# Second layer of a three-layer block: where the first weights and the modulation rows' operands are loaded

## The chip, the cores and the metric

One core of a Trainium2 chip runs the whole program. The time is device microseconds from start to end of one execution; the median of several runs is given, and one further execution is recorded by the hardware profiler. In the text TensorE is PE in the rows, VectorE DVE, ScalarE ACT, GpSimd POOL, and SP is the engine whose queue issues most of the DMAs.

## The reference, cut to what matters

Three layers run one after the other on a sequence of 1024 tokens of width 1024: a layer with two kinds of attention, a layer with latent attention (the one that is edited), and a block whose norms are scaled and shifted by modulation rows, with a mixture of experts at its end. Everything is float32. Of the second layer this is what is computed first:

```python
def mla_layer(x, norm_g, w_in, q_norm, w_uq, kv_norm, w_ukv, w_o, cos, sin):
    h = rms_norm(x, norm_g)
    proj = h @ w_in                                   # 1024 -> 384 + 256 + 32 + 1024
    q_lat, kv_lat, k_rope, gate = split_cols(proj, L1_SIZES)
    q = (rms_norm(q_lat, q_norm) @ w_uq)              # 384 -> 16 heads of 64 + 32
    kv = (rms_norm(kv_lat, kv_norm) @ w_ukv)          # 256 -> 16 heads of 64 + 64
    ...
    return x + (o * jax.nn.silu(gate)) @ w_o
```

The third block begins with

```python
mod = jnp.einsum('bd,de->be', c_act, w_ada[l]) + b_ada[l]
sh1, sc1, g1, sh2, sc2, g2 = [m[:, None, :] for m in jnp.split(mod, N_ADA, axis=-1)]
h = rmsnorm(x, norm_mix_g[l]) * (1.0 + sc1) + sh1
```

## The kernel before, in words

A float32 product is made of three TensorE passes: each operand is split into a rounded part (`_h`, a cast on ScalarE, line 134) and the rest (`_l`, a subtraction on VectorE, line 135), and `mm3` (lines 139 to 141) adds the three products that matter in one PSUM bank. So every weight is loaded to a raw tile, cast, subtracted, and only then used. `load_w` (line 209) does this; with `parts=2` it loads and splits the rows in two halves through one raw tile, so that the second half's DMA waits until the first half is split. With `scale` (lines 227, 228) the split multiplies by a per-row gain.

The order on each engine is set when the program is built: a scheduler goes through the instructions in the order in which the code makes them and, by a model of their times, lets one go ahead whose operands come earlier. So the order on a queue isn't always that of the text. Tiles come from pools; a pool that is opened after another was closed takes the same memory, and the first use of a tile waits for the last use of the tiles that lay there. Most DMAs are issued on SP's queue, in order.

**The step in front** is `out_phase` (line 957), the end of the first layer: for each of 8 tiles of 128 tokens it multiplies by the output weights, adds to the row `x` (line 975), and calls `norm0` (line 1918), which stores `x` (line 1921), norms it (`norm_to_T`, line 246: the normed rows `xn` by VectorE at line 250, eight transposes by TensorE at line 261, the split at lines 134 and 135) and so writes tile t of the hidden state `hT`. Its tiles lie in the pool `c0`.

**The second layer** (`layer1`, line 1034) then opens the pool `lt` in the same memory. It loads the first group of the latents' weights (224 columns of `o_w_in`, tile `wl`, raw tile `wlraw`), then the value weights (`rwv`, lines 1064 to 1078: loaded once for the sum of squares that gives a scale, line 1067, and again to be scaled and split, lines 1076 and 1077). The latents are made in three groups of 224 columns by eight tiles of tokens: `project(c, t)` (line 1081) issues 24 matmuls into one of three PSUM banks, ScalarE sums squares from the bank (line 1085) and VectorE copies it to `lat` (line 1087). The next group's weights are loaded at tile 0 of a group. In the third group `finish(t)` norms and transposes the latents of a tile, and `values(t - 1)` makes the values, which SP stores to `v_d` (line 1125).

When `lt` is closed the pools `w1`, `pq1` (staging of the outputs) and `rq1` follow in its memory. The rotary tables `cosT` and `sinT` are loaded (lines 1145, 1146), and four rounds `c` each load query weights (`wq`, 384 by 256), make two blocks of queries, load key weights (`wk`, 256 by 256), and make two blocks of keys; the first two rounds also make the rotary parts (`rotary`).

Attention follows, head by head (line 1209 and after). Other work is dealt out between its steps by hand: gates up to head 7, half products of the output (`poh`) from head 9 on, bias rows, and from head 5 on in every second step one call of `mod2.run(1, mp)`, which is `total` (line 1306) of `ada_rows`. A modulation row of 1024 is made in four pieces of 256 columns; 24 pieces in all. Their partial sums, 128 rows by 256 columns, were stored to `part_d` long before (line 1304). `total` loads them to `adx` and the bias row to `mb`, sums over the 128 rows with a matmul of ones into the bank that the half products and gates use too, adds the bias, for two of the rows loads a gain into the same `mb` (line 1318) and multiplies, and stores the piece to `mod_d` (line 1320). `adx` and `mb` have one buffer each.

Of the kernel before, what the change touches and what calls it, by code (L numbers as in the profile page):

```python
# [11 lines left out]
F32 = mybir.dt.float32  # L12
# [4 lines left out]
AF = mybir.ActivationFunctionType  # L17
# [1015 lines left out]

def layer1(kk, ps, a, hT, hold, mix_d, gate_d, wo, mod, wx):

# [21 lines left out]
    with kk.pool(name="lt", bufs=1) as lt:  # L1057
        wl = [kk.load_w(lt, W, [(0, 224)], tag="wl", bufs=2, parts=2)]
        lat = lt.tile([P, NT, 672], F32, name="lat")
# [57 lines left out]
        def values(t):  # L1117
# [7 lines left out]
            nc.sync.dma_start(v_d[:, t], v16)  # L1125

        for c in range(3):
            for t in range(NT):
                if t == 0 and c < 2:
                    wl.append(kk.load_w(lt, W, [(224 * (c + 1), 224)], tag="wl", bufs=2, parts=2))  # L1130
                project(c, t)
                if c == 2:
                    finish(t)
                    if t:
                        values(t - 1)
        values(NT - 1)


# [5 lines left out]
    sinT = rq.tile([P, S], F32, name="sinT")  # L1144
    nc.sync.dma_start(cosT, a["c_cos"])
    nc.sync.dma_start(sinT, a["c_sin"])

# [26 lines left out]
    for c in range(4):  # L1174
        w = kk.load_w(wp, a["o_w_uq"], [(256 * c, 256)], nk=3, tag="wq", scale=gq)
        for j in range(2):
            proj_store(kk, ps, pq, w, j * P, P, qT, 3, qn_d, 256 * c + j * P)
        w = kk.load_w(wp, a["o_w_ukv"], [(256 * c, 256)], nk=2, tag="wk", scale=gk)
        for j in range(2):
# [97 lines left out]
def ada_rows(kk, ps, a, mod_d):  # L1277
# [27 lines left out]

    def total(s, z, dst, gname, ap_):
        o = s * D + z * H
        x = ap_.tile([P, H], F32, tag="adx", name=kk.nm("adx"))
        nc.sync.dma_start(x, part_d[:, o:o + H])
        b = ap_.tile([1, H], F32, tag="mb", name=kk.nm("mb"))  # L1310
        nc.sync.dma_start(b, a["b_ada_2"][:, o:o + H])
        pm = ps.tile([P, 512], F32, tag=MM_BANK[0], name=kk.nm("pm"), bufs=MM_BANK[1])
        nc.tensor.matmul(pm[0:1, :H], kk.ones[:, 0:1], x, start=True, stop=True)
        nc.vector.tensor_tensor(x[0:1, :], pm[0:1, :H], b, op=ALU.add)
        if dst == 5:
            nc.vector.tensor_scalar(x[0:1, :], x[0:1, :], 0.5, None, op0=ALU.mult)
        if gname:
            nc.sync.dma_start(b, a[gname][:, z * H:z * H + H])
            nc.vector.scalar_tensor_tensor(x[0:1, :], x[0:1, :], 1.0, b, op0=ALU.add, op1=ALU.mult)
        nc.sync.dma_start(mod_d[dst:dst + 1, z * H:z * H + H], x[0:1, :])  # L1320

    for s, dst, gname in ((1, 0, "norm_mix_g_2"), (0, 1, None), (2, 2, None), (4, 3, "norm_ffn_g_2"), (3, 4, None), (5, 5, None)):
        for z in range(D // H):
            u.add(lambda p, bufs, o=s * D + z * H: unit(o, p, bufs))
        for z in range(D // H):
            v.add(lambda p, s=s, z=z, dst=dst, gname=gname: total(s, z, dst, gname, p))
    return u, v
# [546 lines left out]
def tile_model(ctx: ExitStack, tc: tile.TileContext, a: dict, out: bass.AP, part=None):  # L1874
# [38 lines left out]
    r1 = rx.enter_context(kk.pool(name="r1", bufs=1, side="right"))  # L1913
    hT1 = HL(r1, full, "hT1", tag="hT")
    with kk.pool(name="c0", bufs=1) as op:
        gB = []

        def norm0(t, x):
            if t == 0:
                gB.append(bcast(kk, op, a["o_norm"], D, "gB1"))  # L1920
# [16 lines left out]
    wx = ExitStack()  # L1937
    layer1(kk, ps, a, hT1, hold, mix_d[1], gate_d[1], wo1, (totals, rows), wx)

# [230 lines left out]
```

## Time and profile before

| | |
|---|---|
| median of 3 runs (lowest, highest) | 2584.47 us (2582.06, 2587.52) |
| the profiled execution's own time | 2580.56 us |
| its span in the profile | 2578.8 us |
| TensorE (PE) busy | 2347.5 us, 91% |
| VectorE (DVE) busy | 1834.0 us, 71% |
| ScalarE (ACT) busy | 1379.5 us, 53% |
| GpSimd (POOL) busy | 439.5 us, 17% |
| DMA, mean | 203 GB/s |

Busy time counts an engine's instructions and not what it waits for, and a share over the whole span mixes stages with different limits; TensorE's busy time also grows when its clock is low. So the stages are read one by one, by the chain of work that ended last, the waits and the timelines. The step in front of the second layer ends at about 850 us, its latents and values are done at 963, queries and keys by about 1075, and its attention lasts from there to about 1475.

### The profile page before, as it was taken

Reading aid. Unit: us, or ns where it says so; the run is one execution under the profiler, and the core shown is the slowest. Engines: PE = TensorE matmul, PEld = TensorE weight load, DVE = VectorE, ACT = ScalarE, POOL = GpSimd, SP = SyncE. Lnnn points to the kernel's source line nnn. Section 1 sums busy time; section 2 is a strip of 40 time slices with the busy share of each in tenths; the row PEclk is TensorE's granted clock in tenths of the full one; section 3 lists DMA queues with packets and bytes.
Section 4 is the critical chain, followed back from the end, with each engine's and each line's share of the span. In section 5 each row is a group of like instructions: output and inputs, shape, how many; then the busy total and the mean of one; then the engine's idle time right before and its main releaser. Section 6 shows DMA issues by size and latency. Waiting matters only on the chain.

```text
span 2578.8 us, 41114 instructions
## 1 busy us (share of the span) xinstructions
PE 2347.5 (91%) x14476; PEld 1855.9 (72%) x14476; DVE 1834.0 (71%) x4607; ACT 1379.5 (53%) x2651; POOL 439.5 (17%) x626
## 2 busy tenths in 40 slices
PE   7988888998998888899989989989994999999998
PEld 6866655676787776688767767977873777777776
DVE  4459988876886355366776674767656888888886
ACT  4345675454662333255564466345452767776775
POOL 0000147766750012100000000011000101100110
PEclk9999888898999899999999989989996999999999
DMA  4442476565656226954776461544574999999994
GB/s 131 127 136 79 134 202 183 155 193 165 206 158 204 94 76 254 289 135 118 179 197 174 132 211 51 145 118 140 172 295 188 360 371 365 364 382 367 367 365 142
DMA packets 302637, 523.80 MB, mean 203 GB/s; under 512 B 46022, under 2 KB 191582, under 8 KB 302432
## 3 DMA queue, kind: packets, MB, share of 16 engines
q1 hardware_dynamic: 287456, 467.70, 55.6%
q0 software_dynamic: 14976, 53.49, 6.6%
q8 instruction: 114, 1.87, 0.3%
q14 instruction: 91, 0.75, 0.1%
HBM read 405.18 MB, written 115.65 MB: 202 GB/s over the span
## 4 chain that ended last, share of the span: by engine, by line
PE 61%; DMA 15%; DVE 11%; issue 4%; POOL 4%; ACT 3%; SPq 1%; POOLq 0%; DVEq 0%; ACTq 0%
PE sb L139 6%; PE sb L140 6%; PE sb L141 6%; PE sb L293 5%; DMA adw<-w_ada 4%; PE ptp L340 3%; PE w_gate L1816 2%; PE w_down L139 2%; PE w_down L141 2%; PE w_down L140 2%; PE w_up L1816 2%; DVE tkj L397 2%; PE w_gate L139 2%; PE w_gate L141 2%; PE w_gate L140 2%
## 5 line engine op out<-in xcount | busy, mean ns | idle before, releaser
L341 ACT CAST pTh<-ptp 128x512 f16<-128x512 f32 (+2 forms) x316 | 166.3, 557 | 135.6 <-PE ptp L340 130.1
L342 DVE TENSOR_TENSOR pTl<-ptp,pTh 128x512 f16<-128x512 f32 (+2 forms) x316 | 200.0, 648 | 39.8 <-ACT pTh L341 39.2
L1684 DVE TENSOR_TENSOR ring_l<-mraw,ring_h 128x1024 fp32r<-128x1024 f32 x170 | 203.8, 1221 | 27.6 <-ACT ring_h L1683 27.1
L1683 ACT CAST ring_h<-mraw 128x1024 fp32r<-128x1024 f32 x170 | 174.6, 1047 | 52.9 <-PE w_up L141 22.4
L1684 DVE TENSOR_TENSOR ring_l<-xraw,ring_h 128x1024 fp32r<-128x1024 f32 x150 | 180.2, 1221 | 24.6 <-ACT ring_h L1683 24.0
L340 PE MATMUL ptp<-ident,e 128*128 128x128 f32 x1184 | 182.2, 285 | 5.3 <-ACT e L1574 1.5
L1683 ACT CAST ring_h<-xraw 128x1024 fp32r<-128x1024 f32 x150 | 154.7, 1048 | 40.4 <-PE w_up L141 19.3
L340 PEld LDWEIGHTS ptp<-ident,e 128*128 128x128 f32 x1184 | 133.3, 144 | 18.1 <-issue 4.6
L1247 ACT ACTIVATE e<-e,nmx 128x1024 f32<-128x1024 f32 (+7 forms) x128 | 98.4, 771 | 72.5 <-DVE nmx L1245 72.3
L352 PEld LDWEIGHTS <-pTl 128*128 128x128 f16 x1184 | 107.8, 99 | 35.1 <-issue 16.1
L350 PEld LDWEIGHTS <-pTh 128*128 128x128 f16 x1184 | 109.6, 99 | 31.6 <-issue 21.2
L1773 POOL DMA_INDIRECT xg<-h_d,idx x16 | 24.0, 1501 | 589.8 <-DVE gate L1776 542.3
L1298 POOL TENSOR_SCALAR adw<-adw,ada_s 128x256 f32<-128x256 f32 x192 | 107.1, 569 | 98.8 <-DMA adw<-w_ada 98.3
L902 ACT ACTIVATE e<-e,nmx 128x1024 f32<-128x1024 f32 (+7 forms) x128 | 98.5, 771 | 45.6 <-DVE nmx L901 23.3
L351 PEld LDWEIGHTS <-pTh 128*128 128x128 f16 x1184 | 109.5, 99 | 3.8 <-issue 3.0
L139 PE MATMUL w_down<-ring_h,hTm_h 128*128 128x512 f32 x256 | 105.1, 411 | 0.0
L293 PE MATMUL sb<-hold_l,q 128*128 128x512 f32 (+3 forms) x384 | 102.5, 354 | 1.3 <-DMA q<-qr 1.3
L141 PE MATMUL w_down<-ring_h,hTm_l 128*128 128x512 f32 x256 | 101.1, 395 | 0.0
L140 PE MATMUL w_down<-ring_l,hTm_h 128*128 128x512 f32 x256 | 101.0, 395 | 0.0
L139 PE MATMUL pg<-hold_h,wg_h 128*128 128x512 f32 x192 | 84.7, 441 | 17.5 <-DVE gth L135 15.2
L317 DVE CUSTOM_DVE_ANT_0 e<-sb,hide 128x512 f32<-128x512 f32 (+3 forms) x128 | 74.5, 583 | 34.6 <-PE sb L293 20.6
L139 PE MATMUL w_up<-ring_h,xT_h 128*128 128x512 f32 x192 | 90.3, 470 | 0.0
(590 smaller groups left out, 7626.6 us busy)
## 6 DMA issues: line engine op xcount, KB each, us to landing
mraw<-w_up SPq DMA_DIRECT2D x35, 1024.0 KB
mraw<-w_gate SPq DMA_DIRECT2D x34, 1024.0 KB
mraw<-w_down SPq DMA_DIRECT2D x33, 1024.0 KB
xraw<-w_down SPq DMA_DIRECT2D x30, 1024.0 KB
xraw<-w_gate SPq DMA_DIRECT2D x30, 1024.0 KB
xraw<-w_up SPq DMA_DIRECT2D x29, 1024.0 KB
adw<-w_ada SPq DMA_DIRECT2D x96, 256.0 KB
xh_d<-hx SPq DMA_DIRECT2D x48, 256.0 KB
```

Of the source, the lines that this page charges most:

```text
L139: mm(out, a.hi, b.hi, start=start, stop=False)
L140: mm(out, a.hi, b.lo, start=False, stop=False)
L141: mm(out, a.lo, b.hi, start=False, stop=stop)
L293: mm(sc, a, b[:, k0:k0 + n], start=i == 0, stop=i == len(pairs) - 1)
L340: nc.tensor.transpose(pt[:, j, :], p[:, (g + j) * P:(g + j + 1) * P], kk.ident)
L341: nc.scalar.copy(hi[:, g:g + w, :], pt[:, :w, :])
L342: nc.vector.tensor_tensor(lo[:, g:g + w, :], pt[:, :w, :], hi[:, g:g + w, :], op=ALU.subtract)
L350: mm(out, hi[:, j, :], v1(off + j), start=j == 0, stop=False)
L351: mm(out, hi[:, j, :], v2(off + j), start=False, stop=False)
L352: mm(out, lo[:, j, :], v1(off + j), start=False, stop=j == nb - 1)
L1683: nc.scalar.copy(w.hi, raw_of(i))
L1684: nc.vector.tensor_tensor(w.lo, raw_of(i), w.hi.bitcast(F32), op=ALU.subtract)
```

## The change

The first group of the latents' weights is loaded and split in the step in front, at its tile 2, into tiles of a pool `early` that is opened on the other side of the memory, beside the hidden state, and closed after the last values. The second group is loaded at tile 2 of the first group into tiles of `lt`, the third at tile 2 of the second group into the tiles of `early`; each place holds one weight tile instead of two in `lt`. The first query weights are loaded and split by `queries()` at tile 1 of the third group, into a part of `hold` that is not in use then, through the raw tile of the latents' weights. In the rounds of queries and keys the key weights' load is issued ahead of the query products, and in the first round ahead of the rotary tables. `total` is cut in two: `fetch` issues the loads, with two buffers for `adx` and with the gain beside the bias in `mb`, and `total` of one piece calls `fetch` for the next at its end.

```diff
-def layer1(kk, ps, a, hT, hold, mix_d, gate_d, wo, mod, wx):
+def layer1(kk, ps, a, hT, hold, mix_d, gate_d, wo, mod, wx, wl, early, ex):
...
     with kk.pool(name="lt", bufs=1) as lt:
-        wl = [kk.load_w(lt, W, [(0, 224)], tag="wl", bufs=2, parts=2)]
         lat = lt.tile([P, NT, 672], F32, name="lat")
...
+        def queries():
+            raw = lt.tile([P, 4, 224], F32, tag="wl_raw", name=kk.nm("wqraw")).rearrange("p a b -> p (a b)")[:, 0:768].rearrange("p (k n) -> p k n", n=256)
+            w = HL.view(hold, lambda t: t[:, 5, 0:768].rearrange("p (k n) -> p k n", n=256))
+            nc.sync.dma_start(raw, a["o_w_uq"][:, 0:256].rearrange("(k p) n -> p k n", p=P))
+            for k in range(3):
+                h, l, s = w.hi[:, k, :], w.lo[:, k, :], gq[:, k:k + 1]
+                nc.scalar.activation(h, raw[:, k, :], AF.Copy, scale=s)
+                nc.vector.scalar_tensor_tensor(l, raw[:, k, :], s, h.bitcast(F32), op0=ALU.mult, op1=ALU.subtract)
+            return w
+
         for c in range(3):
             for t in range(NT):
-                if t == 0 and c < 2:
-                    wl.append(kk.load_w(lt, W, [(224 * (c + 1), 224)], tag="wl", bufs=2, parts=2))
+                if t == 2 and c < 2:
+                    wl.append(kk.load_w(early if c else lt, W, [(224 * (c + 1), 224)], tag="wl", parts=2))
+                if (c, t) == (2, 1):
+                    wq0 = queries()
                 project(c, t)
...
         values(NT - 1)
+    ex.close()
...
-    nc.sync.dma_start(cosT, a["c_cos"])
-    nc.sync.dma_start(sinT, a["c_sin"])
...
     for c in range(4):
-        w = kk.load_w(wp, a["o_w_uq"], [(256 * c, 256)], nk=3, tag="wq", scale=gq)
+        w = kk.load_w(wp, a["o_w_uq"], [(256 * c, 256)], nk=3, tag="wq", scale=gq) if c else wq0
+        wk = kk.load_w(wp, a["o_w_ukv"], [(256 * c, 256)], nk=2, tag="wk", scale=gk)
+        if c == 0:
+            nc.sync.dma_start(cosT, a["c_cos"])
+            nc.sync.dma_start(sinT, a["c_sin"])
         for j in range(2):
             proj_store(kk, ps, pq, w, j * P, P, qT, 3, qn_d, 256 * c + j * P)
-        w = kk.load_w(wp, a["o_w_ukv"], [(256 * c, 256)], nk=2, tag="wk", scale=gk)
+        w = wk
...
-    def total(s, z, dst, gname, ap_):
+    rows, loaded = [], {}
+
+    def fetch(i, ap_):
+        if i in loaded or i == len(rows):
+            return
+        s, z, dst, gname = rows[i]
         o = s * D + z * H
-        x = ap_.tile([P, H], F32, tag="adx", name=kk.nm("adx"))
+        x = ap_.tile([P, H], F32, tag="adx", name=kk.nm("adx"), bufs=2)
         nc.sync.dma_start(x, part_d[:, o:o + H])
-        b = ap_.tile([1, H], F32, tag="mb", name=kk.nm("mb"))
-        nc.sync.dma_start(b, a["b_ada_2"][:, o:o + H])
+        b = ap_.tile([1, 2, H], F32, tag="mb", name=kk.nm("mb"))
+        nc.sync.dma_start(b[:, 0], a["b_ada_2"][:, o:o + H])
+        if gname:
+            nc.sync.dma_start(b[:, 1], a[gname][:, z * H:z * H + H])
+        loaded[i] = x, b
+
+    def total(i, ap_):
+        fetch(i, ap_)
+        s, z, dst, gname = rows[i]
+        x, b = loaded[i]
         pm = ps.tile([P, 512], F32, tag=MM_BANK[0], name=kk.nm("pm"), bufs=MM_BANK[1])
         nc.tensor.matmul(pm[0:1, :H], kk.ones[:, 0:1], x, start=True, stop=True)
-        nc.vector.tensor_tensor(x[0:1, :], pm[0:1, :H], b, op=ALU.add)
+        nc.vector.tensor_tensor(x[0:1, :], pm[0:1, :H], b[:, 0], op=ALU.add)
...
         if gname:
-            nc.sync.dma_start(b, a[gname][:, z * H:z * H + H])
-            nc.vector.scalar_tensor_tensor(x[0:1, :], x[0:1, :], 1.0, b, op0=ALU.add, op1=ALU.mult)
+            nc.vector.scalar_tensor_tensor(x[0:1, :], x[0:1, :], 1.0, b[:, 1], op0=ALU.add, op1=ALU.mult)
         nc.sync.dma_start(mod_d[dst:dst + 1, z * H:z * H + H], x[0:1, :])
+        fetch(i + 1, ap_)
...
     hT1 = HL(r1, full, "hT1", tag="hT")
+    wl = []
+    ex = ExitStack()
+    early = ex.enter_context(kk.pool(name="wl0", bufs=1, side="right"))
...
         def norm0(t, x):
+            if t == 2:
+                wl.append(kk.load_w(early, a["o_w_in"], [(0, 224)], tag="wl", parts=2))
             if t == 0:
...
-    layer1(kk, ps, a, hT1, hold, mix_d[1], gate_d[1], wo1, (totals, rows), wx)
+    layer1(kk, ps, a, hT1, hold, mix_d[1], gate_d[1], wo1, (totals, rows), wx, wl, early, ex)
```

## Rows read from the trace of the kernel before

Starts are microseconds from the start of the span. In a timeline row stand the start, the duration, the engine, the line, the operation with its output and inputs, and in brackets how long the engine had been idle before it and what ended that.

**Rows 1.** Chain that ended last, 800 to 1080 us, in order of time: start, length, what.

```profile
847.93 3.61 DMA wlraw<-o_w_in
...
859.71 3.45 DMA wlraw<-o_w_in
...
965.10 6.12 DMA wqraw<-o_w_uq
```

**Rows 2.** Waits of TensorE, 842 to 1080 us: total in us, times, longest.

```profile
PE sb L139 <- ACT wq_h L227: 9.8, 1, 9.8
...
PE pt L261 <- DVE xn L250: 5.0, 2, 3.6
```

**Rows 3.** Timeline of TensorE around the first latents.

```profile
843.15 1.32 PE L261 MATMUL pt<-ident,xn 128*128 128x128 f32 x8 [1.38 <-DVE xn L250]
848.05 1.94 PE L261 MATMUL pt<-ident,xn 128*128 128x128 f32 x8 [3.58 <-DVE xn L250]
852.79 0.56 PE L139 MATMUL sb<-wl_h,hT_h 128*128 128x224 f32 x1 [2.80 <-ACT wl_h L134]
...
868.04 0.37 PE L139 MATMUL sb<-wl_h,hT_h 128*128 128x224 f32 x1 [3.42 <-DVE lat L1087]
```

**Rows 4.** Stretches: length, busy us (instructions) of PE, PEld, DVE, ACT, POOL, clock, DMA, GB/s.

```profile
800.00:834.00 34.00, 34.00 (x177) 28.51 (x177) 28.16 (x65) 12.62 (x23) 0.00 (x0) 1.00 0.63 208
...
845.60:859.20 13.60, 8.21 (x36) 7.57 (x36) 5.42 (x11) 5.54 (x8) 0.00 (x0) 0.50 0.65 224
869.50:872.80 3.30, 3.30 (x18) 3.30 (x17) 1.09 (x1) 0.76 (x3) 0.00 (x0) 0.50 0.18 26
890.00:900.00 10.00, 10.00 (x92) 10.00 (x91) 2.57 (x5) 3.01 (x21) 0.00 (x0) 1.00 0.01 2
...
965.10:975.20 10.10, 3.39 (x8) 2.72 (x9) 2.32 (x7) 2.10 (x5) 0.00 (x0) 0.50 0.70 222
1050.00:1060.00 10.00, 10.00 (x45) 8.06 (x44) 2.52 (x5) 2.35 (x4) 2.82 (x6) 1.00 0.69 257
1205.00:1475.00 270.00, 250.39 (x2396) 196.91 (x2394) 193.60 (x541) 145.42 (x308) 0.00 (x0) 0.98 0.61 164
```

**Rows 5.** Timeline of SP's queue after the last values.

```profile
963.40 0.34 SPq L1125 DMA_DIRECT2D v_d<-v  x1
...
964.26 0.79 SPq L1146 DMA_DIRECT2D sinT<-c_sin  x1
...
965.65 0.49 SPq L220 DMA_DIRECT2D wkraw<-o_w_ukv  x1
```

**Rows 6.** Waits of TensorE, 1205 to 1475 us: total in us, times, longest.

```profile
PE pm L1313 <- DMA adx<-ada_d: 13.8, 9, 2.9
PE pm L1313 <- DVE hx L948: 1.6, 1, 1.6
```

**Rows 7.** Tile `wlraw`: its casts and subtractions, ns shortest, median, longest, first and last start.

```profile
L134 ACT CAST wl_h<-wlraw x6: 929/940/942, 851.8 to 889.3; 128x896 fp32r<-128x896 f32 x6
L135 DVE TENSOR_TENSOR wl_l<-wlraw,wl_h x6: 1091/1092/1094, 852.8 to 890.2; 128x896 fp32r<-128x896 f32 x6
```

**Rows 8.** Timeline of VectorE, 863 to 871 us.

```profile
864.16 1.09 DVE L135 TENSOR_TENSOR wl_l<-wlraw,wl_h 128x896 fp32r<-128x896 f32 x1 [2.89 <-ACT wl_h L134]
865.21 2.48 DVE L1077 SCALAR_TENSOR_TENSOR hold_l<-rwv,gks,hold_h 128x1024 fp32r<-128x1024 f32 x2
867.61 0.98 DVE L1087 COPY lat<-sb 128x224 f32<-128x224 f32 x3
869.84 1.09 DVE L135 TENSOR_TENSOR wl_l<-wlraw,wl_h 128x896 fp32r<-128x896 f32 x1 [1.26 <-ACT wl_h L134]
```

**Rows 9.** The sums' matmuls: ns shortest, median, longest, first and last start.

```profile
L1313 PE MATMUL pm<-adx,ones x48: 376/377/634, 1211.5 to 1464.6; 128*1 128x256 f32 x48
```

**Rows 10.** Waits of SP's queue, 1205 to 1475 us: total in us, times, longest.

```profile
SPq L1309 <- DMA mod_d<-adx: 31.9, 21, 4.0
```

**Rows 11.** The partial sums' tile in memory: us from a DMA's issue to its landing.

```profile
DMA to landing us min/median/max: 2.0/3.3/7.1
```

More of the change, by code (lines that the diff above doesn't have):

```diff
@@ L1325, in ada_rows @@
         for z in range(D // H):
-            v.add(lambda p, s=s, z=z, dst=dst, gname=gname: total(s, z, dst, gname, p))
+            v.add(lambda p, i=len(rows): total(i, p))
+            rows.append((s, z, dst, gname))
     return u, v
```

## The prediction

> **What bounds the kernel now.** I read the page first (TensorE is busy nine tenths of the span, the table above), then the chain that ended last around the code that is edited, then TensorE's waits in the same stretches, then the timelines of the engines and of SP's queue at each gap. What the reader should see is that TensorE stands still, or runs at its lower clock, in three places that the edit touches, and hardly anywhere else nearby.
>
> First place, the start of the second layer. The chain leaves TensorE after the last transposes of the step in front and runs through the load of the latents' weights, its casts, the second group's load and the copy of a latent out of PSUM [rows 1]. TensorE's waits there are 5.0 us for the last normed rows [rows 2], 2.8 us for the first cast and 3.4 us for the copy of a latent out of PSUM [rows 3]. The timeline gives the positions: the first latent matmul starts at 852.79, seventy-two matmuls (three PSUM banks of 24) are issued, and the seventy-third starts only at 868.04 [rows 3]. At full clock 92 such matmuls go into 10 us [rows 4], so the seventy-two are 7.8 us of work and took 15.3 us.
>
> Second place, the first queries: one wait of 9.8 us for the cast of their weights [rows 2]. Their load goes out at 965.10 and needs 6.1 us [rows 1], because on SP's queue it comes behind the values' store and two rotary tables [rows 5].
>
> Third place, the second layer's attention from its sixth head on. TensorE is busy 250.4 of 270 us there, VectorE 193.6, ScalarE 145.4 [rows 4]. TensorE's longest wait by far is 13.8 us, nine times, in the sum over a modulation row's partial sums (line 1313), for their load; the next is 1.6 us [rows 6].
>
> **The clock** is part of each price. In 845.6 to 859.2, 869.5 to 872.8 and 965.1 to 975.2 the granted clock is 0.50, the 1.2 GHz level, each time after a gap in TensorE's work; in the attention stretch the mean is 0.98 of 2.4 GHz [rows 4].
>
> **A. Latents.** Removed: the first group's load from the start of the layer (two halves, each 3.6 us to land, 0.94 us of cast on ScalarE, 1.09 us of subtraction on VectorE [rows 1, 7]). It stood there because its raw tile shared memory with the step in front and was asked for at 847.93, the moment that step's last normed row was done. With the weights in tiles of their own, TensorE can start on tiles 0 to 5 of the hidden state while it waits for tiles 6 and 7. Between its transposes it is free for 3.6 us before 848.05 and 1.4 us before 843.15 [rows 3]: 5.0 us, or 45 matmuls. The transposes end at 850.0; the 27 that are left of the three banks take 2.9 us, to 852.9. That is 15.1 us before 868.04. The second low-clock stretch (3.4 us at half speed, 1.7 us lost) has no cause left: upper bound 16.8 us. Moving the second group's load from tile 0 to tile 2 also matters: now VectorE does that group's subtraction at 864.16 and the value weights' at 865.21 before it copies the first latent [rows 8], and the PSUM banks stay full that long.
> Lower bound: the copies still stand behind the value weights on VectorE. Their own loads can't start before 847.9 (same memory); 3.6 us to land, two squares (2.7), 2.0 for the scale, a second load (3.6), and two casts and subtractions (2.2 to the first, 1.3 to the second, overlapped) end near 862. Then the gain is 6.0 + 1.7 = 7.7 us. I take 14 us. It is nearer to the upper end because the queues are not in the order of the text: in [rows 8] a subtraction that is written after the value weights' runs before them, so work goes where its operands are expected.
>
> **B. First queries.** Their load, three casts and three subtractions move into the third group of latents, into the buffer half that nothing uses there. TensorE goes from the last value matmul straight to the queries: 9.8 us, and of the low clock in 965.1 to 975.2 the 3.4 us after 971.8 in which it worked cost 1.7: upper bound 11.5 us. What is late next is the key weights. Now issued fourth at 965.65, they go first, right behind the store at 963.40 [rows 5]; an estimate of 3.6 us as for the latents' half, and some 1 us of splitting, gives 968.5. The queries are 36 matmuls at 45 in 10 us [rows 4], 8 us, to 970.3: covered. If the keys' weights land as late as now, or the outputs' staging tiles must wait for the values' store, up to 4.5 us come back: lower bound 7. The rotary tables come after these loads and are wanted only after queries and keys, some 13 us on. I take 11 us.
>
> **C. Modulation rows.** 24 sums stand 11 us apart (1211.5 to 1464.6 over 23 steps [rows 9]). Before, the next load could not be issued until the previous row's store had landed: SP waited 31.9 us in 21 times for that [rows 10]. Now there are two buffers, and the load goes out right after the previous sum. A load lands in 2.0 to 7.1 us [rows 11], so 11 us cover even the longest. Gone: 13.8 us of TensorE, and 2% of 270 us, 5.4, if the clock holds: upper bound 19. Lower bound 2: the sum still shares one PSUM bank with the half products of the output (the 1.6 us row of [rows 6]), and VectorE, at 72%, may become what ends the next step. I take 13, the wait alone: the other waits of that list are near 1 us each, so little else is queued up behind it.
>
> **D. Costs.** The early group's 2.2 us of VectorE and 1.9 of ScalarE lie in a stretch where TensorE is busy 34.0 of 34.0 us and VectorE 28.2 [rows 4]; the 6 us that VectorE has left cover it. The queries' split adds 1.3 us to ScalarE in the third group. The second and third groups' loads start two tiles later and take 11 us (asked for at 859.71 [rows 1], split at 870.9 [rows 8]), against 16 us of matmuls left in the group. The number of DMAs is unchanged. On SP the second half of the early load waits for the first half's split, some 5.5 us, and the step's own loads and stores stand behind it; they are asked for a tile (6.8 us) ahead. 0 to 5 us; I take 2.
>
> **Sum:** 14 + 11 + 13 - 2 = 36 us. The profiled execution took 2580.56 us (span 2578.8 and 1.8 around it); 2544.6 after. The median shown is 3.9 us above that execution, so I forecast 2548.5.
>
> **The rivals.**
> R1, the latents start early but their copies stay behind the value weights: A is 7.7, the time 2554.8. For it: [rows 8]; against: the order there follows readiness.
> R2, the sums' wait only changes its name (the shared bank, VectorE): C is 2, the time 2559.5. For it: VectorE's 72%; against: the short list in [rows 6].
> R3, the early load holds up the step in front. Its halves take 3.6 us each [rows 1]; if the operands of a tile queue behind both, TensorE, which has no idle time there, loses up to 7.2 us once: 2555.7. The Trainium skill (DMA: Bandwidth & Descriptors, section Queues, rings and completion order) says that descriptors issued by SP are consumed in ring order on each DMA engine, which speaks against putting a large load there; no row before shows such a collision, and by this rule the sum would be 28.8 instead of 36.
> R4, the new tiles' memory is itself not free before the step in front ends, so that the load goes out at 847.9 as now: A is 1, the time 2561.5. Against: the side they are put on holds only the hidden state in that step.
> R5, slower. The prefetch is issued by SP right behind a sum, and its row of the bias has one buffer, so SP waits in order for VectorE; the next head's loads stand behind it. SP waited 1.5 us on average at this place before [rows 10] without TensorE losing time on head loads. If 24 such waits reach TensorE, C turns from 13 gained into 36 lost, 49 us against a gain of 36: 2597.5. It decides from 1 us per sum on (23 us from A, B and D over 24).
>
> **How the numbers follow.** Forecast 0.50, R1 0.20, R2 0.13, R3 0.05, R4 0.04: all faster, 0.92. R5 0.05. All parts given back by a changed order elsewhere, 0.03 for no change. "No change" means within 0.2%, 5.2 us, about what a measurement of this kernel can tell. The range takes all upper bounds (16.8 + 11.5 + 19 = 47.3 us) to all lower ones (7.7 + 7 + 2 - 5 = 11.7): 2537 to 2573, rounded down by 1 at each end. It holds the forecast and R1 to R4.
>
> **What would show it.** A: latent matmuls between the last transposes, none waiting for a cast of their weights, the granted clock at 1.00 where it was 0.50, the seventy-third near 853. B: no wait for the queries' cast, the first query matmul under 1 us after the last value matmul. C: no wait of line 1313 for its load. R3 would show as waits of the step in front for its operands, R5 as waits of the score matmuls for head loads. The prediction is wrong if the latents' copies or the staging tiles stop TensorE for over 10 us in the same stretches, or if attention keeps its 270 us.

## The result, and the profile after

The changed kernel takes 2552.07 us (median of 4 runs, 2548.09 to 2557.46); the kernel before, measured beside it, 2583.26 us (4 runs). The ratio is 0.9882, with a 95% interval of 0.986 to 0.9903. Measured once more on another occasion ("again", below) it is 0.9864 (0.9844 to 0.9883); one run of the kernel before took 2704.14 us there at a lower clock and is not counted. So some 31 to 35 us are gone, 36 were forecast, and the forecast of 2548.5 us is 3.6 us below the median. The parts did not come out as forecast, though; that is what the rest is about.

The page of the changed kernel, first part: busy time, share of the span (2550.8 us) and instructions of each engine.

```profile
PE 2337.4 (92%) x14476; PEld 1848.9 (72%) x14476; DVE 1836.8 (72%) x4607; ACT 1378.5 (54%) x2651; POOL 443.6 (17%) x626
```

TensorE's busy time is 10 us less than before, although it has the same matmuls to do: part of the work now runs at the higher clock (mean granted clock 0.952 in this execution, 0.947 before).

**The first latents.** TensorE's timeline of the changed kernel, where [rows 3] stood before:

```profile
831.27 1.04 PE L261 MATMUL pt<-ident,xn 128*128 128x128 f32 x8
832.06 0.35 PE L139 MATMUL sb<-wl_h,hT_h 128*128 128x224 f32 x1
...
840.49 0.60 PE L261 MATMUL pt<-ident,xn 128*128 128x128 f32 x4
841.03 0.60 PE L261 MATMUL pt<-ident,xn 128*128 128x128 f32 x4
...
843.39 0.37 PE L139 MATMUL sb<-wl_h,hT_h 128*128 128x224 f32 x1 [1.31 <-DVE lat L1086]
```

The first latent matmul (832.06) follows the transposes of the sixth tile at once, and the latents go on between the transposes of the last two tiles. The last transposes wait for nothing any more, and the seventy-third latent matmul (843.39) comes 2.0 us after the last transpose, where it came 18.5 us after it. All of TensorE's waits between 780 and 955 us:

```profile
PE sb L139 <- ACT hold_h L134: 4.6, 7, 0.7
PE ptl L1108 <- ACT lat L1092: 2.4, 2, 1.2
PE sb L139 <- DVE lat L1086: 1.3, 1, 1.3
PE sb L139 <- DVE pst_l L135: 1.0, 1, 1.0
PE sb L139 <- DVE v L1123: 0.5, 1, 0.5
```

The waits for the normed rows and for the weights' cast [rows 2, 3] are not in this list. The stretches of the changed kernel, with the columns of [rows 4]:

```profile
832.06:843.39 11.33, 10.02 (x92) 9.83 (x90) 7.75 (x18) 5.36 (x15) 0.00 (x0) 1.00 0.55 173
843.39:887.00 43.61, 41.80 (x369) 41.34 (x370) 18.60 (x54) 18.16 (x62) 2.29 (x12) 1.00 0.20 61
887.40:890.80 3.40, 3.40 (x16) 3.23 (x15) 0.67 (x3) 0.61 (x1) 0.00 (x0) 0.50 0.00 0
...
955.70:959.10 3.40, 3.40 (x8) 2.74 (x9) 2.24 (x5) 1.12 (x2) 0.53 (x1) 0.50 0.72 236
976.00:983.00 7.00, 3.50 (x8) 2.81 (x9) 1.98 (x3) 0.66 (x2) 1.11 (x2) 0.51 1.00 404
```

The granted clock is 1.00 through the first two groups of latents, where it was 0.50 twice; 3.4 us at 0.50 come in the third group. In the queries and keys the low clock has not gone: its stretches lie elsewhere than before.

**Queries and keys.** TensorE's waits from 936 to 1065 us in the changed kernel:

```profile
PE sb L139 <- DVE pst_l L135: 12.2, 5, 5.9
PE pg L139 <- DVE gth L784: 3.7, 2, 3.0
```

The 9.8 us for the queries' weights [rows 2] are gone. In their place stands a wait for a staging tile's subtraction, 12.2 us; in the same stretch the kernel before lost 6.7 us to it. ScalarE's timeline shows what is late behind it:

```profile
945.41 1.56 ACT L134 CAST pst_h<-sb 128x512 fp32r<-128x512 f32 x3 [3.88 <-DMA v_d<-v]
...
952.57 1.07 ACT L134 CAST pst_h<-sb 128x512 fp32r<-128x512 f32 x2 [2.83 <-DMA qn_hi<-pst_h]
...
975.00 1.07 ACT L134 CAST pst_h<-sb 128x512 fp32r<-128x512 f32 x2 [1.50 <-DMA qr<-qrs_h]
980.00 0.59 ACT L134 CAST pst_h<-sb 128x512 fp32r<-128x512 f32 x1 [3.93 <-DMA qr<-qrs_h]
```

Each block of queries or keys is cast into one of two staging tiles and stored from there (by GpSimd's queue, not SP's). The rotary rows (`qrs`) go through the same two tiles and are stored to `qr`. The first cast waits for the values' store (the tiles lie in the same memory), the later ones for the stores of what was in their tile before: the block two before at 952.57, the rotary rows at 975.00 and 980.00.

**Attention.** TensorE's waits from 1185 to 1470 us, where [rows 6] stood, and below it the wait of SP's queue that answers to [rows 10]:

```profile
PE pt L1010 <- DMA mxt<-mix_d: 4.5, 1, 4.5
PE pv L352 <- DVE pTl L342: 4.1, 4, 2.1
PE ptp L340 <- ACT e L1262: 3.7, 1, 3.7
PE pv L350 <- ACT pTh L341: 2.2, 3, 1.1
PE pm L1342 <- DVE brs L800: 1.3, 1, 1.3
PE pm L1342 <- DMA adx<-ada_d: 1.0, 1, 1.0
```

```profile
SPq L1329 <- DMA mod_d<-adx: 34.4, 18, 3.4
```

The wait for the partial sums fell from 13.8 to 1.0 us, but other waits, 14.5 us in all by the first four lines, now stand in the list; of the same kinds the kernel before had 2.7 us in its attention and 0.5 us (`mxt`) right behind it. Of these, the score matrix's exponentials (`e`), their casts (`pTh`) and the rest (`pTl`) are the attention's own chain through ScalarE and VectorE; `mxt` is the first operand of the closing step, which waits for the last head's store. The attention did not get shorter: from head 5's product with the values to the last head's last product it takes 250.8 us, 247.9 before. What fills it is work that used to follow (below).

### The profile page after: what moved, and what is told of

It is laid out like the page before. It is cut to its first block, busy times and chain, and to the rows that moved or that the text cites. A ratio compares the mean times of both kernels' runs of the same rounds, so it can differ in the third digit from the quotient of the medians.

```text
span 2550.8 us, 41148 instructions
## 1 busy us (share of the span) xinstructions
PE 2337.4 (92%) x14476; PEld 1848.9 (72%) x14476; DVE 1836.8 (72%) x4607; ACT 1378.5 (54%) x2651; POOL 443.6 (17%) x626
## 4 chain that ended last, share of the span: by engine, by line
PE 62%; DMA 14%; DVE 11%; issue 5%; POOL 4%; ACT 3%; SPq 1%; POOLq 0%; DVEq 0%; ACTq 0%
PE sb L139 6%; PE sb L140 6%; PE sb L141 6%; PE sb L293 5%; PE ptp L340 3%; DMA adw<-w_ada 3%; PE w_gate L1846 2%; PE w_down L139 2%; PE w_down L141 2%; PE w_down L140 2%; PE w_up L1846 2%; DVE tkj L397 2%; PE w_gate L139 2%; PE w_gate L141 2%; PE w_gate L140 2%
## 5 line engine op out<-in xcount | busy, mean ns | idle before, releaser
L340 PE MATMUL ptp<-ident,e 128*128 128x128 f32 x1184 | 181.0, 284 | 12.1 <-ACT e L1262 3.7
```

Of the source, the lines that this page charges most:

```text
L340: nc.tensor.transpose(pt[:, j, :], p[:, (g + j) * P:(g + j + 1) * P], kk.ident)
```

## The experiments

The program's first layer and its third block run at a clock that varies from execution to execution (the low-clock time of the first layer alone was 91 to 116 us), so a profiled execution's total says little about a few us. The table therefore gives, beside the ratio of the times to the kernel before (measured side by side; the quotient of the two medians differs from it by up to 0.0011), three stretches of each profiled execution: S1, from the last transpose of the step in front to the last latent matmul; S2, from there to the first head's product with the values; S3, from head 5's to the router of the third block, with TensorE's idle time in it (length less busy time). All are read from timelines and stretches. In the expectations, the "last normed rows' transposes before the second layer" are those of the sixth tile, the 831.27 above.

| kernel | ratio to before (95%) | S1 | S2 | S3 | idle in S3 |
|---|---|---|---|---|---|
| before | 1 | 102.9 | 148.7 | 660.5 | 53.3 |
| a_only: part A alone | 0.9924 (0.9902, 0.9946) | 85.4 | 152.4 | 655.7 | 52.0 |
| a_t0: A, later loads at tile 0 | 0.9937 (0.9914, 0.9961) | 85.5 | 151.8 | 662.8 | 54.0 |
| b_only: part B alone | 0.9983 (0.9971, 0.9995) | 102.6 | 145.9 | 660.8 | 53.7 |
| b_st0: B and a third staging tile | 0.9951 (0.9931, 0.9971) | 105.4 | 139.0 | 652.8 | 51.3 |
| c_only: part C alone | 0.9971 (0.9956, 0.9986) | 105.9 | 151.0 | 653.8 | 48.4 |
| c_buf: C's second buffers alone | 0.9983 (0.9964, 1.0003) | 102.2 | 151.6 | 655.6 | 48.1 |
| the changed kernel | 0.9882 (0.986, 0.9903) | 87.1 | 146.4 | 659.0 | 48.9 |
| again: the same | 0.9864 (0.9844, 0.9883) | 85.4 | 149.2 | 648.8 | 49.2 |
| a_held: early load held back | 0.9875 (0.9849, 0.9901) | 85.4 | 140.1 | 655.4 | 47.9 |
| s_pad: staging tiles elsewhere | 0.9888 (0.9869, 0.9906) | 85.5 | 149.1 | 652.8 | 47.3 |
| s_st0: a third staging tile | 0.9881 (0.9862, 0.9899) | 85.5 | 143.1 | 651.3 | 47.9 |
| tail: half products held back | 0.9922 (0.9906, 0.9938) | 85.5 | 146.8 | 658.0 | 49.0 |
| best: held load, third tile | 0.9897 (0.9873, 0.9921) | 85.4 | 144.4 | 653.5 | 48.8 |

The stretches scatter too. S2 is 148.7 to 152.4 us in the five kernels without part B (mean 151.1), though their code there is the same, and S1 is 102.2 to 105.9 in the five without part A.

**The three parts alone.** Each is the kernel before with that part of the diff.

> The first group of latents' weights early, and the later groups' loads at tile 2; queries and modulation rows as before. Theory (the parts add up; A is worth what the trace shows between the last transposes and the second group): from the end of the step in front to the 193rd latent matmul 16 to 17 us less than before, and all of the stretch from the last latent to the first head unchanged within 2 us; the whole 16 to 25 us less, by whether the 9 us that the changed kernel's trace shows less in the first layer come with this part (its order of work there is changed, because the load and its split went out near 605 us, in the first layer). Rival 1 (VectorE's copies stay late): under 8 us. Rival 2 (the first layer's 9 us are chance between two executions): 16 us less in time, and no lasting difference in the first layer.

> Only the first query weights' early split and the new order of loads in the first round. Theory from the changed kernel's trace: the wait of 9.8 us for the cast is gone, but about 7 us return as TensorE's wait for the subtraction into the staging tiles (12 us in that trace against 6.7 before), so 2 to 5 us less in the whole. Rival (as predicted, covered): 9 to 11 us less. Second rival (the return belongs to the combination with the latents' part): 9 us here too.

> Only the modulation rows' prefetch. As predicted: the 13.8 us of TensorE's waits gone and 13 us less in the whole. Theory from the changed kernel's trace: the waits for the load go from 13.8 to about 1 us, but TensorE's idle time from the sixth head to the router falls by only some 4 us, and the low-clock stretches there decide the rest: 0 to 6 us less. The first layer, whose order is the same as before, has the time of before; if its trace is again 5 us or more shorter, that difference is chance.

Measured: 0.9924, 0.9983 and 0.9971, that is about 20, 4 and 7 us. Their product, 0.9878, agrees with the changed kernel's two ratios within their intervals: the parts add. A shortens S1 by 17.5 us, B shortens S2 by 2.8, C takes 4.9 us out of TensorE's idle time in S3.

**The early load held back.** In the changed kernel the load stands in the code at tile 2 of the step in front, but the scheduler issued it at 604.7 us, in the first layer's attention, and with it changed the order of the instructions there. Here it is tied to the store of tile 1 on SP's queue, and it goes out at 802.1:

```diff
             if t == 2:
-                wl.append(kk.load_w(early, a["o_w_in"], [(0, 224)], tag="wl", parts=2))
+                with kk.tc.issue_after(gB[1]):
+                    wl.append(kk.load_w(early, a["o_w_in"], [(0, 224)], tag="wl", parts=2))
```

> The changed kernel, but the early load may not be issued on SP before the store of the rows of tile 1 of the step in front, so that the first layer's order is the same as before. If the first layer's 9 us come from the load's place in it, this kernel is 6 to 10 us slower than the changed one (ratio 0.991 to 0.993 against before instead of 0.988). If they are chance, it is as fast as the changed kernel within 3 us. If a load of 0.46 MB in the step in front holds up its operands (the rival of the prediction), TensorE's waits there grow by up to 7 us.

0.9875, and S1 as in the changed kernel: A's gain does not hang on the place of the load. With the load inside the step in front, TensorE's only waits from 785 to 863 us were these:

```profile
PE sb L139 <- ACT mT_h L134: 2.2, 1, 2.2
PE sb L139 <- DVE lat L1086: 1.5, 1, 1.5
```

None is for a load; the first comes at 785.72, ahead of the early load, and the second is that of the seventy-third latent matmul.

**The changed kernel again, and the tile of the later loads.** The second is part A alone with one character changed:

```diff
-                if t == 2 and c < 2:
+                if t == 0 and c < 2:
```

> The changed kernel itself, once more, so that the three kernels that go with it have it on the same chip. All theories: 0.988 of the kernel before, within 0.002. Its profile is a second look at the same program, and says what of the differences between profiled executions is chance: if the first layer again ends at 831 us (the last normed rows' transposes before the second layer), the 9.5 us by which it ended earlier than in the kernel before belong to the program; if it ends anywhere between 828 and 841, they are chance of the clock.

> Part A alone, but with the second and third group's weights loaded at tile 0 of a group as in the kernel before, not at tile 2; the first group's early load and the tiles of their own stay. Theory 1 (R1 of the prediction: what fills the start is decided by VectorE's order; a second group's split at tile 0 stands ahead of the latents' copies and stops TensorE when three banks are full): from the last normed rows' transposes to the seventy-third latent matmul it takes over 17 us instead of the 12.1 of part A alone (27.3 before), and the ratio is 0.994 to 0.9965 against 0.9924. Theory 2 (only the first group's early load matters; the scheduler places the later loads and splits by itself): 12 to 14 us, ratio 0.9915 to 0.9935.

In "again" the sixth tile's transposes come at 835.25: within the bounds for chance, which speaks against a gain of the full 9.5 us in the first layer. In a_t0 S1 is 85.5 us, the seventy-third latent matmul starts again 2.0 us after the last transpose (12.1 us after the sixth tile's transposes, as in a_only), and it waits for the same thing as in the changed kernel:

```profile
845.11 0.37 PE L139 MATMUL sb<-wl_h,hT_h 128*128 128x224 f32 x1 [1.31 <-DVE lat L1086]
```

On VectorE the copies of the first latents stand ahead of the value weights in both kernels; the scheduler puts them there whichever tile the load is written at. So the early first group, in tiles of its own, is all of A, and the move of the later loads is worth nothing that can be measured. The ratios (0.9937 and 0.9924) agree within their intervals.

**Staging tiles: place or number.** Two kernels made from the changed one. The first puts 5.5 KB of unused memory (in each of the 128 rows) ahead of the staging tiles; the second gives the first round a third tile.

```diff
     wp = px.enter_context(kk.pool(name="w1", bufs=2))
+    gap = px.enter_context(kk.pool(name="gap", bufs=1))
+    gap.tile([P, 1408], F32, name="gap")
```

```diff
+    s0 = rp.enter_context(kk.pool(name="st0", bufs=1))
...
-            proj_store(kk, ps, pq, w, j * P, P, qT, 3, qn_d, 256 * c + j * P)
+            proj_store(kk, ps, pq if c or j else s0, w, j * P, P, qT, 3, qn_d, 256 * c + j * P)
...
-            proj_store(kk, ps, pq, w, j * P, P, kT, 2, kn_d, 256 * c + j * P)
+            proj_store(kk, ps, pq if c or not j else s0, w, j * P, P, kT, 2, kn_d, 256 * c + j * P)
```

> The changed kernel with 5.5 KB of unused memory put between the weights' pool and the staging tiles of queries and keys, so that the first staging tiles no longer lie over the values' tiles; still two staging buffers. Theory 1 (part B is given back because the first staging cast waits 3.9 us for the values' store, and the queue of casts behind it slides): that wait is gone, TensorE's wait for the staging subtraction falls from 12.2 us to under 7.8, the stretch from the last latent matmul to the first head falls by 3 to 6 us, ratio 0.986 to 0.987. Theory 2 (it is given back because two staging buffers wait for their own stores of 2 to 3 us each, wherever they lie): TensorE's wait stays at 8 to 12 us, the stretch changes by less than 2 us, ratio as of the changed kernel within 0.001.

> The changed kernel with a third staging tile for the first round of queries and keys (first block of queries and second block of keys), in memory that the values' tiles do not touch. Theory 1 (place): the same as with the unused memory, 3 to 6 us less between the last latent matmul and the first head. Theory 2 (number of buffers): 4 to 8 us less there, TensorE's wait for the staging subtraction under 5 us, ratio 0.985 to 0.986, and more gain than the unused memory gives by itself. Neither (DMA queues full between 950 and 970 us, where the changed kernel's DMA share is 0.93 to 0.98): no change in that stretch, the waits move to the loads of the second round's weights.

s_pad, ScalarE's timeline and, below it, TensorE's wait from 925 to 1075 us:

```profile
937.96 0.59 ACT L134 CAST pst_h<-sb 128x512 fp32r<-128x512 f32 x1
...
949.26 1.07 ACT L134 CAST pst_h<-sb 128x512 fp32r<-128x512 f32 x2 [4.25 <-DMA qn_hi<-pst_h]
```

```profile
PE sb L139 <- DVE pst_l L135: 15.5, 4, 6.6
```

The first cast waits for nothing now, and the third block waits longer for the first one's store: TensorE's wait grew from 11.9 us (again, on the same chip) to 15.5, and S2 is the same. So the place is not the cause; a theory that a single wait in the timeline had suggested falls. s_st0, the same wait from 929 to 1072 us:

```profile
PE sb L139 <- DVE pst_l L135: 5.5, 3, 2.9
```

S2 is 6.1 us shorter than in "again" and 3.3 shorter than in the changed kernel's first profile. But the ratios (0.9881 against 0.9864) show no gain: 6 us are 0.24%, less than the width of an interval.

**Part B alone with the third tile** asks the same where nothing else has changed.

> Part B alone with a third staging tile in the first round of queries and keys. Theory (the 11 us forecast for part B were given back because two staging buffers wait for their stores): TensorE's wait for the staging subtraction falls from 12.2 us to about 5.5, as in the changed kernel with the third tile, the stretch from the last latent matmul to the first head from 145.9 us to about 140, ratio 0.9955 to 0.9965 against 0.9983 of part B alone. Rival (the give-back is the lower clock and the full DMA queues, not the staging tiles): wait down, but the stretch stays at 144 to 148 us and the ratio at 0.9975 to 0.999.

b_only, then b_st0, TensorE's wait in S2:

```profile
PE sb L139 <- DVE pst_l L135: 12.2, 4, 6.4
```

```profile
PE sb L139 <- DVE pst_l L135: 4.4, 4, 1.7
```

The wait is 7.8 us shorter, S2 6.9, and the ratio goes from 0.9983 to 0.9951, about 8 us; B with three staging tiles gains 12.6 us by its ratio and 9.7 in S2. The forecast for B was 11. As the two intervals just touch, the stretch is the stronger evidence: 139.0 us lies well below the 148.7 to 152.4 of the kernels without B, and 145.9 only a little.

Why two tiles cost less before: the time from issue to landing of the staging tiles' stores (`pst_h`, shortest, median, longest) in the first round, of the kernel before (978 to 1000 us) and of b_only (960 to 985):

```profile
DMA to landing us min/median/max: 3.6/4.3/6.2
```

```profile
DMA to landing us min/median/max: 5.2/7.2/8.2
```

And the pause of the kernel before, as a stretch with the columns of [rows 4]:

```profile
964.00:971.80 7.80, 0.00 (x0) 0.00 (x0) 0.01 (x1) 0.55 (x2) 0.00 (x0) 0.57 0.93 310
```

TensorE did nothing in it, but the DMA engines were 93% busy: rotary tables and weights went through. Now they go through beside the stores (in b_only the tables are issued at 964.47 and 965.29, the first block's store at 965.94), and the stores land 3 us later. The same holds in every profile: the high parts of the first two blocks land after 3.0 to 3.9 us in the five kernels without B and after 5.0 to 8.0 us in the nine with it. That it is these loads that slow the stores is read from the order of issue and not tested. A busy DMA by itself does not tell the two apart: while the first store of the kernel before landed in 3.6 us (980.4 to 984.0), the DMA engines were as fully busy (a share of 1.01).

**The end of the attention.** In the changed kernel the half products run earlier than before. Their matmuls, nanoseconds (shortest, median, longest), first and last start, before and after:

```profile
L139 PE MATMUL poh<-hT_h,mT_h x64: 389/396/503, 1355.8 to 1488.1; 128*128 128x512 f32 x64
```

```profile
L139 PE MATMUL poh<-hT_h,mT_h x64: 389/396/496, 1291.6 to 1433.6; 128*128 128x512 f32 x64
```

The last head's last product starts at 1470.0 before and at 1446.6 after, so before, 48 matmuls stood behind it and covered the store and load of `mix_d`; after, none. To test whether that is where C's gain went, four half products (48 matmuls) are held back:

```diff
-            if (h, i) in HALF1_AT:
+            if (h, i) in HALF1_AT[:12]:
...
-    halves.run()
+    with kk.tc.issue_after(end):
+        halves.run()
```

(`HALF1_AT` lists the steps at which a half product is dealt out; `end` is the last matmul of `pv_mm`, the product with the values.)

> The changed kernel with the last four half products of the output (48 matmuls, some 11 us) held on TensorE until after the last head's last product, where the kernel before has them too; the sums stay as in the changed kernel. Theory (part C is partly given back at the end of the attention: the half products that used to cover the last store and load of the mixed rows have moved forward into the time that the sums no longer need, so TensorE waits 4.5 us there and runs some 7 to 10 us at the lower clock after it): the wait for the mixed rows falls below 1 us, the low-clock stretch that begins 3 to 4 us after the last head is gone, the time from head 5 to the router falls by 4 to 8 us, ratio 0.985 to 0.9865. Rival (the wait only marks the end of a chain on ScalarE and VectorE, which sets the end of the attention): the wait goes, but the attention ends later by as much as was taken out of it less 1 to 2 us, and the stretch from head 5 to the router changes by less than 2 us.

TensorE's waits of this kernel from 1195.6 to 1505 us:

```profile
PE ptp L340 <- ACT e L1263: 5.2, 4, 3.2
PE pv L352 <- DVE pTl L342: 3.1, 4, 1.9
PE pt L1011 <- DVE gtt L1012: 2.6, 1, 2.6
PE pt L1011 <- DMA mxt<-mix_d: 2.2, 2, 1.8
```

The wait for the mixed rows falls from 4.5 to 2.2 us and the attention is 10 us shorter (239.0 us from head 5 to its last product, 249.1 in "again"), but what was taken out of it now follows it: idle time in S3 is 49.0 us, as in "again" (49.2). The theory falls; covering that wait uncovers others. By its ratio this kernel is even slower than "again" by 0.6%. S3 is 9.2 us longer than in "again" and about as long as in the changed kernel's first profile, so the profiles do not settle it; why stays open.

**The second buffer alone.** The kernel before with `bufs=2` for `adx` and `mb`, and nothing loaded ahead by the sum before.

```diff
-        x = ap_.tile([P, H], F32, tag="adx", name=kk.nm("adx"))
+        x = ap_.tile([P, H], F32, tag="adx", name=kk.nm("adx"), bufs=2)
...
-        b = ap_.tile([1, H], F32, tag="mb", name=kk.nm("mb"))
+        b = ap_.tile([1, H], F32, tag="mb", name=kk.nm("mb"), bufs=2)
```

> The kernel before with two buffers each for a modulation row's partial sums and bias, and nothing else of the change: no load issued ahead by the sum before, gain still loaded in the sum itself. Theory 1 (the second buffer is what takes the wait away; the scheduler issues the load early by itself): TensorE's wait for the partial sums' load falls from 13.8 us to under 3, the sums come early as in part C alone, ratio 0.996 to 0.9985. Theory 2 (the explicit early load is needed): the wait stays over 6 us, ratio 0.9985 to 1.0005. Either way, if TensorE's idle time from head 5 to the router falls by less than half of what the wait for the partial sums loses, the rest of the gain forecast for C went into other waits.

TensorE's waits of it from 1217 to 1540 us:

```profile
PE pt L261 <- ACT xn L1955: 8.2, 2, 7.0
PE pt L1010 <- DMA mxt<-mix_d: 4.5, 1, 4.5
PE pm L1313 <- DMA adx<-ada_d: 4.2, 2, 3.8
PE ptp L340 <- ACT e L1247: 3.7, 3, 2.3
```

The wait is 4.2 us, a little above what theory 1 named, and the idle time in S3 (48.1 us) is as low as with all of C (48.4). The buffer does it; the early load takes away 3 us of a wait and nothing measurable of the time. The wait fell by 9.6 us here and by 12.8 in c_only, and in both the idle time fell by 5 us. The longest idle time of ScalarE in c_only's attention shows one of the things that stand behind it: a cast of output weights that waits for its load holds up the casts and exponentials behind it in ScalarE's order, and TensorE waits for those.

```profile
1357.50 1.15 ACT L918 ACTIVATE hT_h<-woraw,gv 128x1024 fp32r<-128x1024 f32 x1 [8.18 <-DMA woraw<-o_w_o]
1360.20 1.12 PE L340 MATMUL ptp<-ident,e 128*128 128x128 f32 x4 [4.35 <-ACT e L1247]
```

**Held load and third tile together.**

> The changed kernel with the early load of the latents' weights held on SP until the step in front has stored its second tile of rows, and with the third staging tile. If the two pieces add in the medians as they did in the stretches of the profiles (staging tile: 6 us less between the last latent matmul and the first head; the held load: no difference), the ratio is 0.9845 to 0.9865, against 0.9882 and 0.9864 of the changed kernel's two measurements. If the staging wait only hides another limit, 0.9865 to 0.988.

0.9897 (0.9873 to 0.9921): no better than the changed kernel, and outside both ranges expected. The 2 to 5 us that S2 is shorter cannot be told from nothing in the ratios; it is even longer than with the held load alone (144.4 against 140.1 us). No kernel tried here beats the changed one.

## Why the prediction was right, and where it was not

The sum of 36 us and the sign hold. Of the parts, A gave more than forecast, B and C less, and some 4 to 10 us of the total belong to none of them. So the mechanisms are right for A and for the waits that went, but that the total comes within 4 us of the forecast is luck. Two of the prediction's own signs of being wrong did come: the staging tiles stop TensorE for 12.2 us in the queries and keys, and the attention keeps its length.

**A (forecast 14, bounds 7.7 and 16.8): about 16.** From the sixth tile's transposes to the last latent matmul it took 111.8 us before (840.73 to 952.48) and 95.5 after in "again" (835.25 to 930.78) and in a_only (827.70 to 923.20); in the first profile 97.2, as 3.4 us of low clock fell into the third group. The steps are those forecast: latents between the last transposes, no wait for the cast, clock 1.00. The waits account for 9.9 us of it (5.0, 2.8 and 3.4 before, 1.3 after) and the clock for about 6, an estimate from S1's length before, 102.9 us, and its mean granted clock, 0.94 before and 1.00 in "again". The step that failed is that moving the later loads to tile 2 mattered: a_t0 shows that it doesn't, because the scheduler had already put the copies first, and so R1 did not come.

**B (forecast 11, bounds 7 and 11.5): about 4,** 0.9983 alone, below its lower bound, though the interval (1 to 7.5 us) just reaches it; S2 is 2.8 us shorter than before, and 3.6 if the means of five kernels without B and five with it and two tiles are compared (151.1 and 147.5). The 9.8 us went as forecast. The step that failed is the lower bound: it did name the staging tiles' wait for the values' store, but priced it at 4.5 us at most, as a thing that happens once. s_pad shows that this one wait is beside the point, and b_st0 what is at it: each block waits for the store of the block two before, and these stores now land later; that the tables and weights, which used to move in the pause, are the reason is likely and not tested. The prediction called the tables harmless because they are wanted late; what they slow down was not asked. With a third tile B alone gives what was forecast.

**C (forecast 13, bounds 2 and 19): about 5 by the idle time, 7 by the ratio.** The wait for the partial sums went as forecast (13.8 to 1.0). The step that failed is the reason given for 13 rather than less: "the other waits of that list are near 1 us each, so little else is queued up behind it". A list of waits shows what came last, not what comes next. Over all profiled executions TensorE's idle time in S3 was 51.3 to 54.0 us in five kernels without C and 47.3 to 49.2 in nine with C's buffers: 4.5 us less. By the idle time R2 (the wait changes its name, 2 us left) was nearer than the forecast. The shared bank did not take over; VectorE did in part, with the attention's own chain and the start of the closing step. In S3 TensorE waits for VectorE's `pTl` in line 352 for 0.6 to 1.4 us in the kernels without C and for 4.1 to 4.9 in eight of the nine with it (1.5 in c_buf), and for `mxt` for 0 to 1.0 us and for 4.5 to 4.6 in eight of nine (2.2 in tail). That these waits are what the removed one turned into is read from the lists; the one attempt to take a link out (tail) changed the list and not the idle time.

**D (2).** The step in front takes 1 to 2 us longer between its first output matmul and its last transpose (61.9 us before, 63.2 in the changed kernel, 63.4 in "again"), with sixty-eight latent matmuls more in it and 5 us of waits less. R3, the early load in the way of the step's operands, does not show in a_held, where the load does go out inside the step. The Trainium skill (DMA: Bandwidth & Descriptors, section Queues, rings and completion order) states that each DMA engine consumes descriptors in ring order; in a_held, where operands of the step were issued on SP behind this load (`mxt` at 802.57, the load at 802.10), TensorE has no wait for them in the list above. R4 did not come: the load was free to go out 240 us early. R5 did not come either: SP waits longer at the sums than before (34.4 us against 31.9, in order for their stores), but from head 5 on the scores wait for a head's load no more than 1.5 us in any profile.

**What was not forecast.** 16, 4 and 5 make 25 us, and the medians say 31 to 35; with 7 for C it is 27. By the profiled executions, some of the rest lies in the first layer. TensorE's order there is one in seven kernels (before, b_only, b_st0, c_only, c_buf, and the two with the held load) and another in the seven in which the early load is issued at 600 to 606 us. From TensorE's first instruction to the step in front the first take 768.0 to 775.2 us (mean 771.7), the second 762.0 to 769.9 (mean 766.2). That would be 5.5 us for a changed order that nobody intended. But two executions of one order lie as far apart (768.0 us in c_only, 775.2 in the kernel before), and the ratios of the kernels with the held load (0.9875, 0.9897) are not apart from the others (0.9864, 0.9882, 0.9881), so this is left open; the rest is within the intervals.

## What to carry to other kernels

When a load's wait is taken away, ask what else moved in the pause, and whether the consumer's output buffers empty fast enough beside it; the pause may have been what kept two buffers enough. A wait in a list is no price for its removal: of 13 us in the attention, where three engines pass work around in turn, about a third came back, while in the latents, where the clock was low behind the waits, 10 us of waits brought 16. Where a scheduler orders the instructions, where a load is written can matter less than which memory it has: in C the second buffer alone took as much idle time away as the whole part, and in A neither the tile of the later loads nor holding the early load back by 200 us changed anything that could be measured.

## What the runs showed that was not expected

The first layer took 763 to 770 us in five profiled executions of the changed kernel and kernels made from it that share its order, with 93 to 112 us at the low clock, so a single profile can't settle a change of under 8 us there. A load written into the step in front was issued 174 us before that step began (604.7 against 778.2), and with it the order of an attention changed that it has nothing to do with. And in a_held, S2 was 9 us shorter than in "again" without a change of that stretch's matmuls: on SP's queue all four stores of the rotary rows had come ahead of a load of query weights that lay between them in "again", and TensorE's wait for the staging tiles was 7.8 us instead of 11.9. That the one is the reason for the other was not tested.
